# DeltaNet on one core: head results transposed behind later projections, gates ahead of projections, pieces of products between the last merges

## The chip, the cores and the metric

The kernel runs on one core of a Trainium2 chip. The metric is the device time of one execution in microseconds (us). One execution was also recorded by the hardware profiler; line numbers such as L1378 are lines of the kernel before unless the text says that they are of the changed one. Engines: PE multiplies matrices, DVE works on vectors, ACT on functions and copies, POOL is the third elementwise engine, SP issues the DMAs.

## The reference, cut to what matters

The program is two blocks of a network on 256 tokens with a context of 256 more. The change lies in one layer, a gated delta rule ("DeltaNet") with 8 key heads, each with 2 value heads, in two directions of time:

```python
def project(h):
    p = h @ w_in
    qkv = silu(short_conv_2(p[..., :DN_QKV_DIM], conv_w))
    z = p[..., DN_QKV_DIM:DN_QKV_DIM + DN_V_DIM]
...
def step(s, xs):                       # gated_delta_rule, one chunk
    m = where(strict, bc[..., :, None] * kk * decay, 0.0)
    sol = triangular_solve(eye + m, rhs, lower=True, unit_diagonal=True)
...
def readout(o, z):
    o = rms_norm_2(swapaxes(o, 1, 2), norm_g)
    o = o * silu(z.reshape(bsz_, n, DN_V_HEADS, DN_HEAD_V))
    return o.reshape(bsz_, n, DN_V_DIM) @ w_out
```

So each head needs four projections (q and k in one tile, two value parts), two gates `z`, the inverse of a unit triangular matrix, a recurrence over chunks, a normalised and gated result, and a product with its part of `w_out`.

## The kernel before, in words

Everything of this layer is in the function `deltanet`. All products with weights take three matmuls per 128 input channels (`mm3`, L310 to L318): weight and activation are each split in a high and a low part, and high by high, high by low and low by high are added in PSUM. A weight of 1024 by 128 therefore makes 24 matmuls of 512 columns. `weight` (L298) loads it by DMA, ACT casts the high part (L307), POOL in this layer subtracts to get the low part (L308).

The pieces of a head are:
- `project(hd)` (L1140): four products of 24 matmuls. ACT and DVE apply a convolution of 5 taps straight from PSUM (L1148, L1153), ACT a SiLU.
- `gates(hd)` (L1159): two products of 24 matmuls, which only ACT reads, with a SiLU, into `z`.
- `prepare(hd)` (L1169): transposes of k, products of k and q (L1200), decay products (L1209, L1210) that ACT exponentiates into `D` (L1214), and `Mt`. `Mt` goes through DRAM (`din`), DVE inverts blocks of 16 by substitution (L1239, L1240), ACT copies (`XX`, L1241), and the blocks go through DRAM (`dout`, L1247) into `TT` (L1255).
- `tokens` (L1259): transposes of q and of two value tiles.
- `merge(hd)` (L1282): three levels of two halves, each of three groups of four 128-column products (L1297, L1303, L1308) with a copy by ACT (L1294) and DVE work between, which grow the blocks of the inverse to 128.
- `steps(hd)` (L1312): four steps of two directions, with the results in two tiles `ot`.
- `readout` (L1367): ACT squares `ot` (L1372), DVE takes an inverse square root by integer guess and three rounds (`rsqrt`, L416 to L422) and scales `ot` (L1378); PE transposes `ot` in two groups of four (L436, called from `transpose`), DVE multiplies by `z` (L1384), and `pair` splits the product into high and low parts (L294, L295).
- `write_out(hd)` (L1388): eight products of 6 matmuls, whose results DVE adds to the tokens (`finish`, L641).

A scheduler of the framework sets the order of instructions of each engine from the order in which the code issues them and from their dependences; each engine then runs its own list in order. `issue_after(x)` puts all PE instructions of its block behind the instruction x in PE's list. The main loop (L1409) is a software pipeline: while head hd goes through its steps, the preparation of hd+1 and the projections of hd+2 are on their way. PSUM has eight banks, which this layer shares as three rings (L1801): `b` for transposes and preparation, `a` for merges and steps, `mm` for products with weights.

## Time and profile before

| what | value |
|---|---|
| three runs, us | 2682.57, 2691.01, 2696.7 (median 2691.01) |
| profiled execution, us | 2684.89 |
| its span, us | 2683.1 |
| busy share of the span | PE 94%, PEld (weight loads of PE) 79%, DVE 61%, ACT 42%, POOL 14% |
| mean granted clock of TensorE | 0.971 of full speed |
| DMA | 334.09 MB, mean 125 GB/s |

The median is of separate runs; the trace belongs to the profiled execution, whose span is 1.8 us shorter than its device time. A row of a timeline gives the start in us from the start of the span, the duration, the engine, the line, what was written from what, the sizes, how many instructions were put together, and in brackets how long the engine had stood idle before and what released it. The DeltaNet layer is in the middle of the span; a matmul of PE is pipelined, so that one of 0.39 us can be followed by the next after 0.23 us.

### The profile page before, as it was taken

What the parts mean: (1) busy time and instruction counts of PE and PEld (TensorE: products, weight loads), DVE (VectorE), ACT (ScalarE), POOL (GpSimd) and SP (SyncE); (2) the same over time, 40 slices, a digit from 0 to 9 for tenths busy, and PEclk for the clock granted to TensorE, in tenths of its full rate; (3) what the DMA queues carried; (4) which work ended last, traced back from release to release, by engine and by line L of the source; (5) the groups of instructions that cost most, each with busy time, mean ns of one, the idle gap of its engine ahead of it and who ended that gap; (6) DMA issues with size and microseconds to landing.
All of it is one profiled execution on the core that took longest, in us unless ns stands there. A gap on an engine that the chain in (4) does not pass through costs nothing.

```text
span 2683.1 us, 40564 instructions
## 1 busy us (share of the span) xinstructions
PE 2515.0 (94%) x15740; PEld 2117.8 (79%) x15740; DVE 1640.5 (61%) x3455; ACT 1133.2 (42%) x2159; POOL 363.2 (14%) x268
## 2 busy tenths in 40 slices
PE   7999999999999899879899989987999999798999
PEld 4866877778887899757787778776877888698999
DVE  4554443334576778777866786776533435777675
ACT  3344333222454455544444444433422324564453
POOL 0000200000100100232223323222000001410100
PEclk8999999999999899889999999999999999899999
DMA  7334476662241565222112211211544522231554
GB/s 263 124 121 141 165 276 243 237 241 87 82 128 60 169 192 182 72 58 59 35 51 63 58 48 54 64 43 48 195 162 169 181 91 71 77 95 58 179 182 157
DMA packets 147105, 334.09 MB, mean 125 GB/s; under 512 B 57134, under 2 KB 68512, under 8 KB 146912
## 3 DMA queue, kind: packets, MB, share of 16 engines
q1 hardware_dynamic: 146656, 331.43, 37.9%
q8 instruction: 124, 2.03, 0.3%
q14 instruction: 69, 0.57, 0.1%
q0 software_dynamic: 256, 0.07, 0.0%
HBM read 327.78 MB, written 3.67 MB: 124 GB/s over the span
## 4 chain that ended last, share of the span: by engine, by line
PE 74%; DVE 16%; ACT 3%; issue 3%; DMA 2%; POOL 1%; SPq 1%; DVEq 0%; POOLq 0%; ACTq 0%
PE pmm L316 18%; PE pmm L317 17%; PE pmm L318 17%; PE pmd L378 3%; DVE lf L1239 2%; PE ps L986 1%; PE pa L1303 1%; PE pmm L335 1%; DVE wl L308 1%; DVE rsy L422 1%; DMA wm<-wmod 1%; PE pa L1350 1%; PE pmm L336 1%; PE pmm L334 1%; PE pv L1024 1%
## 5 line engine op out<-in xcount | busy, mean ns | idle before, releaser
L307 ACT CAST wh<-wr 128x1024 fp32r<-128x1024 f32 (+1 forms) x421 | 426.4, 1017 | 740.7 <-PE pmm L317 537.6
L316 PE MATMUL pmm<-h,wh 128*128 128x512 f32 (+2 forms) x1800 | 630.7, 350 | 25.0 <-DVE kq L1153 13.9
L318 PE MATMUL pmm<-h,wl 128*128 128x512 f32 (+2 forms) x1800 | 626.4, 348 | 16.5 <-DVE wl L308 12.1
L317 PE MATMUL pmm<-h,wh 128*128 128x512 f32 (+2 forms) x1800 | 625.1, 347 | 0.0
L308 DVE TENSOR_TENSOR wl<-wr,wh 128x1024 fp32r<-128x1024 f32 (+1 forms) x333 | 394.7, 1187 | 302.2 <-ACT wh L307 295.7
L316 PE MATMUL pmm<-r,wh 128*128 128x256 f32 (+1 forms) x1312 | 445.1, 340 | 7.2 <-DVE rst L420 3.9
L318 PE MATMUL pmm<-r,wl 128*128 128x256 f32 (+1 forms) x1312 | 444.9, 340 | 5.4 <-DVE wl L308 5.3
L317 PE MATMUL pmm<-r,wh 128*128 128x256 f32 (+1 forms) x1312 | 445.7, 340 | 2.2 <-DVE r L295 2.1
L308 POOL TENSOR_TENSOR wl<-wr,wh 128x1024 fp32r<-128x1024 f32 x88 | 214.2, 2437 | 1428.4 <-ACT wh L307 817.0
L316 PEld LDWEIGHTS pmm<-h,wh 128*128 128x128 f32 x1800 | 348.0, 193 | 74.4 <-issue 24.3
L318 PEld LDWEIGHTS pmm<-h,wl 128*128 128x128 f32 x1800 | 348.5, 194 | 59.8 <-DVE wl L308 13.3
L317 PEld LDWEIGHTS pmm<-h,wh 128*128 128x128 f32 x1800 | 348.8, 194 | 37.2
L316 PEld LDWEIGHTS pmm<-r,wh 128*128 128x128 f32 x1312 | 248.7, 190 | 41.2 <-issue 13.2
L318 PEld LDWEIGHTS pmm<-r,wl 128*128 128x128 f32 x1312 | 249.3, 190 | 32.2 <-DVE wl L308 6.7
L317 PEld LDWEIGHTS pmm<-r,wh 128*128 128x128 f32 x1312 | 249.6, 190 | 26.2 <-DVE r L295 2.8
L641 DVE SCALAR_TENSOR_TENSOR xs<-pmm,modb,xs 128x256 f32<-128x256 f32 x232 | 106.3, 478 | 135.1 <-PE pmm L318 134.9
L641 DVE SCALAR_TENSOR_TENSOR xs<-pmm,moda,xs 128x256 f32<-128x256 f32 x120 | 54.4, 480 | 149.0 <-PE pmm L318 148.9
L294 ACT CAST r<-h 128x256 fp32r<-128x256 f32 (+1 forms) x128 | 65.6, 514 | 127.0 <-DVE h L594 67.3
L295 DVE TENSOR_TENSOR r<-h,r 128x256 fp32r<-128x256 f32 (+1 forms) x128 | 72.9, 570 | 43.3 <-ACT r L294 39.9
L378 PE MATMUL pmd<-wm,cvs 128*32 128x256 f32 x1408 | 87.7, 384 | 0.3 <-DMA wm<-wmod 0.3
L378 PEld LDWEIGHTS pmd<-wm,cvs 128*32 128x32 f32 x1408 | 41.2, 110 | 40.7 <-issue 14.2
L334 PE MATMUL pmm<-h,wh 128*128 128x256 f32 x224 | 64.6, 295 | 5.4 <-ACT h L499 3.5
(483 smaller groups left out, 3784.9 us busy)
## 6 DMA issues: line engine op xcount, KB each, us to landing
wr<-w SPq DMA_DIRECT2D x128, 512.0 KB
wr<-f SPq DMA_DIRECT2D x128, 512.0 KB
wm<-amod SPq DMA_DIRECT2D x24, 2048.0 KB
wr<-dwin SPq DMA_DIRECT2D x49, 512.0 KB
wm<-wmod SPq DMA_DIRECT2D x12, 2048.0 KB
wr<-win SPq DMA_DIRECT2D x28, 512.0 KB
wm<-wmod SPq DMA_DIRECT2D x8, 1536.0 KB
wr<-gwin SPq DMA_DIRECT2D x17, 512.0 KB
```

What stands on the lines that cost most here:

```text
L294: self.nc.scalar.copy(hi, src)
L295: self.nc.vector.tensor_tensor(lo, src, hi.bitcast(F32), ALU.subtract)
L307: self.nc.scalar.copy(hi, raw)
L308: (self.nc.gpsimd if pool or self.pool_lo else self.nc.vector).tensor_tensor(lo, raw, hi.bitcast(F32), ALU.subtract)
L316: mm(ps, wh[:, k, :], rh[:, n0:n1], start=k == 0, stop=False)
L317: mm(ps, wh[:, k, :], rl[:, n0:n1], start=False, stop=False)
L318: mm(ps, wl[:, k, :], rh[:, n0:n1], start=False, stop=k == last)
L334: mm(ps[:, c0:c1], wh[:, k, :], rh[:, c0:c1], start=k == 0, stop=False)
L335: mm(ps[:, c0:c1], wh[:, k, :], rl[:, c0:c1], start=False, stop=False)
L378: self.last = nc.tensor.matmul(ps[32 * c : 32 * c + 32, :256], cs[:, k + i, :], raw[:, i, 256 * c : 256 * c + 256], start=k + i == 0, stop ...
L641: self.nc.vector.scalar_tensor_tensor(x, ps, mod[:, 8 * gch + m, v : v + 1], x, ALU.mult, ALU.add)
L1239: nc.vector.tensor_tensor(p3, N3[:, i : i + 1, 0:i].to_broadcast([P, i, i]), X[:, 0:i, 0:i].rearrange("p j c -> p c j"), ALU.mult)
```

## The change

The change has four parts.

1. `readout` is cut in two. `scale` (squares, square root, scaling of `ot`) is called where `readout` was; the rest, from the transposes on, is called after `project(hd + 2)`, and `issue_after` puts it behind the last matmul of that projection. For head 6, which has no such projection, it stands behind the first gate product of head 7, for head 7 behind the last pieces of part 3.
2. `gates(0)` comes ahead of `tokens` and `project(1)`.
3. For head 7 the second gate product and the whole of `write_out(6)` become 24 pieces of 3 matmuls (`lin_parts`, `late`). `between` issues one piece behind the first product group of each of the six half levels of the merge and behind each direction of steps 0 to 2, two behind each direction of step 3, and the rest follows the steps.
4. The PSUM rings change from b=3, a=3, mm=2 to b=2, a=3, mm=3.

```diff
--- before.py
+++ after.py
@@ -315,13 +315,29 @@
         for k, (rh, rl) in list(enumerate(rhs))[k0:k1]:
             mm(ps, wh[:, k, :], rh[:, n0:n1], start=k == 0, stop=False)
             mm(ps, wh[:, k, :], rl[:, n0:n1], start=False, stop=False)
-            mm(ps, wl[:, k, :], rh[:, n0:n1], start=False, stop=k == last)
+            self.mark = mm(ps, wl[:, k, :], rh[:, n0:n1], start=False, stop=k == last)
 
     def lin(self, src, rhs, n0, n1, w=None, pool=False):
         w = w or self.weight(src, pool=pool)
         ps = self.mm_ps()
         self.mm3(ps[:, : n1 - n0], w, rhs, n0, n1)
         return ps[:, : n1 - n0]
+
+
+    def lin_parts(self, w, rhs, n, use):
+        ps = self.mm_ps()[:, :n]
+        w = w()
+        for k in range(len(rhs)):
+            yield lambda: self.mm3(ps, w, rhs, 0, n, k, k + 1)
+        use(ps)
+
+    def between(self, parts, ins, n=1):
+        for _ in range(n):
+            part = next(parts, None)
+            if part is None:
+                return
+            with self.tc.issue_after(ins):
+                part()
 
 
     def lins(self, ws, rhs, streams, tag="mm"):
@@ -1156,14 +1172,32 @@
                     vf.append(acc)
             return kq, vf
 
+
+        def gate(hd, j):
+            ps = self.lin(win[5 + 6 * hd + j], h, 0, 512)
+            z = ap.tile([P, 512], F32, tag="z" if hd < 7 else "vf", bufs=2, name="z")
+            nc.scalar.activation(z, ps, AF.Silu)
+            return z
+
         def gates(hd):
-            zs = []
-            for j in range(2):
-                ps = self.lin(win[5 + 6 * hd + j], h, 0, 512)
-                z = ap.tile([P, 512], F32, tag="z", bufs=2, name="z")
-                nc.scalar.activation(z, ps, AF.Silu)
-                zs.append(z)
-            return zs
+            return [gate(hd, 0), gate(hd, 1)]
+
+
+        def late(zs, og):
+            def use(ps):
+                zs.append(ap.tile([P, 512], F32, tag="vf", bufs=2, name="z"))
+                nc.scalar.activation(zs[1], ps, AF.Silu)
+
+            yield from self.lin_parts(lambda: self.weight(win[48]), h, 512, use)
+            ws = [self.weight(a["dwout"][6, mq]) for mq in range(2)]
+            for m in range(8):
+                c = slice(P * (m % 4), P * (m % 4) + P)
+
+                def use(ps):
+                    for s2 in st:
+                        self.finish(xs, m, ps[:, s2[0] : s2[1]], mod, 2, s2, None, None)
+
+                yield from self.lin_parts(lambda: [w[:, :, c] for w in ws[m // 4]], og, 512, use)
 
         junk = lambda: ap.tile([P, P], F32, tag="junk", bufs=1, name="junk")
 
@@ -1279,7 +1313,7 @@
             c["vt"] = vt
 
 
-        def merge(hd, c):
+        def merge(hd, c, parts):
             Mt, TT = c["Mt"], c["TT"]
 
             def mix(t, p, np_, s):
@@ -1294,7 +1328,8 @@
                     nc.scalar.copy(v4(FT), mix(TT[1], 4 * hf, 4, s))
                     py = self.a_ps()
                     for p in range(4):
-                        mm(py[:, C(p)], Mt[:, 2 * hf + p // 2, p % 2], mix(TT[0], 4 * hf + p, 1, s), start=True, stop=True)
+                        i = mm(py[:, C(p)], Mt[:, 2 * hf + p // 2, p % 2], mix(TT[0], 4 * hf + p, 1, s), start=True, stop=True)
+                    self.between(parts, i.ins)
                     Y = ap.tile([P, 512], F32, tag="Y", bufs=2, name="Y")
                     nc.vector.tensor_tensor(Y.rearrange("p (a i) -> p a i", a=4), py.rearrange("p (a i) -> p a i", a=4),
                                             lm[:, lv].unsqueeze(1).to_broadcast([P, 4, P]), ALU.mult)
@@ -1305,11 +1340,11 @@
                         nc.vector.tensor_tensor(o, o, v4(py), ALU.subtract)
                     pzt = self.a_ps()
                     for p in range(4):
-                        mm(pzt[:, C(p)], Y[:, C(p)], FT[:, C(p)], start=True, stop=True)
+                        i = mm(pzt[:, C(p)], Y[:, C(p)], FT[:, C(p)], start=True, stop=True)
                     nc.vector.tensor_tensor(mix(TT[1], 4 * hf, 4, s), v4(FT), v4(pzt), ALU.subtract)
 
 
-        def steps(hd, c):
+        def steps(hd, c, parts):
             kq, vt, D, mbt, ktm, TB = c["kq"], c["vt"], c["D"], c["mbt"], c["ktm"], c["TT"][1]
             S = None
             ot = [ap.tile([P, 512], F32, tag="ot", bufs=2, name="ot") for _ in range(2)]
@@ -1347,7 +1382,8 @@
                     if step:
                         mm(pks[:, 256:], ks(1), S[:, 256 * d : 256 * d + 256], start=True, stop=True)
                     for v in range(2):
-                        self.mark = mm(ptr[:, 256 + P * v : 384 + P * v], D[ch][:, 2 * d + v], vA[:, C(v)], start=True, stop=True)
+                        i = mm(ptr[:, 256 + P * v : 384 + P * v], D[ch][:, 2 * d + v], vA[:, C(v)], start=True, stop=True)
+                    self.between(parts, i.ins, 2 if step == 3 else 1)
                     o = ot[ch // 2][:, 256 * (ch % 2) : 256 * (ch % 2) + 256]
                     if step:
                         tq = self.e()
@@ -1364,7 +1400,7 @@
                 S = Sn
             return ot
 
-        def readout(c, ot, zs):
+        def scale(c, ot):
             ss = sp.tile([P, 4, 2], F32, tag="ss", name="ss")
             jk = junk()
             for ch in range(4):
@@ -1376,6 +1412,8 @@
             for p in range(2):
                 o = ot[p].rearrange("p (c i) -> p c i", i=P)
                 nc.vector.tensor_tensor(o, o, so[:, 4 * p : 4 * p + 4].unsqueeze(2).to_broadcast([P, 4, P]), ALU.mult)
+
+        def readout(ot, zs):
             og = []
             for v in range(2):
                 pt = self.b_ps()
@@ -1402,29 +1440,36 @@
                     then(sv)
 
         c = prepare(0, *project(0))
+        zs = gates(0)
         tokens(c)
         proj = project(1)
-        zs = gates(0)
-        og = None
+        og, parts = None, iter(())
         for hd in range(8):
-            merge(hd, c)
-            ot = steps(hd, c)
             if hd == 7:
-                zs = gates(hd)
+                parts = late(zs, og)
+            merge(hd, c, parts)
+            ot = steps(hd, c, parts)
             if hd < 7:
                 nxt = prepare(hd + 1, *proj)
-            if hd == 7:
-                with self.tc.issue_after(self.mark.ins):
-                    write_out(6, og)
-            elif hd > 0:
+            if 0 < hd < 7:
                 write_out(hd - 1, og)
             if hd < 7:
                 tokens(nxt)
-            og = readout(c, ot, zs)
+            scale(c, ot)
+
             if hd < 6:
                 proj = project(hd + 2)
+            elif hd == 6:
+                zn = [gate(7, 0)]
+            else:
+                for part in parts:
+                    part()
+            with self.tc.issue_after(self.mark.ins):
+                og = readout(ot, zs)
             if hd < 6:
                 zs = gates(hd + 1)
+            elif hd == 6:
+                zs = zn
             if hd < 7:
                 c = nxt
         S = dict(acc={}, new=lambda n: ap.tile([P, 512], F32, tag="FT", bufs=2, name="acc")[:, :n],
@@ -1798,7 +1843,7 @@
                 f = dict(h=self.norm_mod(xs, both, gs, mods2[0][0], 0, [y[:, :2], y[:, 2:]], "sq", self.hr()),
                          ws=[self.weight(a["dwin"][m]) for m in range(2)])
         with ExitStack() as st:
-            self.pools(st, dict(g=3, e=(5, 256)), dict(b=3, a=3, mm=2), 4, "b", pool_lo=True)
+            self.pools(st, dict(g=3, e=(5, 256)), dict(b=2, a=3, mm=3), 4, "b", pool_lo=True)
             self.dn = st.enter_context(self.tc.tile_pool(name="dn", bufs=1))
             h = self.deltanet(xs, mods2[0][0], f["h"], f["ws"], [both[0], both[1]] if skip else [both[1], both[0]])
         S = {}
```

The lists of PE show where instructions go. The lines of the changed kernel are other numbers: L452 is L436 of before, L1331, L1338 and L1343 are L1297, L1303 and L1308, and L316 to L318 are the same. Names: `pmm<-h` is a projection or gate product, `pmm<-r` one of `write_out`, `pb<-k_id,ot` a transpose of the result, `pa<-TT,Mt` the first group of a half level of a merge.

PE at the end of head 1, before. The 31 projection matmuls of which the last four stand here follow the last transposes of `vf`:

```order
L316 MATMUL pmm<-h,wh 128x512
L317 MATMUL pmm<-h,wh 128x512
L318 MATMUL pmm<-h,wl 128x512
L316 MATMUL pmm<-h,wh 128x512
L436 MATMUL pb<-k_id,ot 128x128 x4
L317 MATMUL pmm<-h,wh 128x512
L436 MATMUL pb<-k_id,ot 128x128 x4
L318 MATMUL pmm<-h,wl 128x512
L316 MATMUL pmm<-h,wh 128x512
```

The same place, changed:

```order
L316 MATMUL pmm<-h,wh 128x512
L317 MATMUL pmm<-h,wh 128x512
L318 MATMUL pmm<-h,wl 128x512
L452 MATMUL pb<-k_id,ot 128x128 x8
L316 MATMUL pmm<-h,wh 128x512
L317 MATMUL pmm<-h,wh 128x512
L318 MATMUL pmm<-h,wl 128x512
L316 MATMUL pmm<-h,wh 128x512
```

What moved: the two groups of four transposes are eight in a row, and 96 projection matmuls instead of 31 stand between them and the steps.

PE between steps(0) and merge(1), before. Behind the steps come 55 projection and gate matmuls, the transposes of `ot`, and 15 more, of which the last three stand here:

```order
L316 MATMUL pmm<-h,wh 128x512
L317 MATMUL pmm<-h,wh 128x512
L318 MATMUL pmm<-h,wl 128x512
L1297 MATMUL pa<-TT,Mt 128x128 x4
L436 MATMUL pb<-k_id,kq 128x128 x4
L1200 MATMUL pb<-kq 128x256
L1303 MATMUL pa<-Y,FT 128x128 x4
L1308 MATMUL pa<-FT,Y 128x128 x4
```

The same place, changed. Behind the steps come 10 matmuls, of which the last three stand here:

```order
L316 MATMUL pmm<-h,wh 128x512
L317 MATMUL pmm<-h,wh 128x512
L318 MATMUL pmm<-h,wl 128x512
L1331 MATMUL pa<-TT,Mt 128x128 x4
L1338 MATMUL pa<-Y,FT 128x128 x4
L1343 MATMUL pa<-FT,Y 128x128 x4
L1331 MATMUL pa<-TT,Mt 128x128 x4
L1338 MATMUL pa<-Y,FT 128x128 x4
L1343 MATMUL pa<-FT,Y 128x128 x4
L1331 MATMUL pa<-TT,Mt 128x128 x4
L452 MATMUL pb<-k_id,ot 128x128 x8
L1338 MATMUL pa<-Y,FT 128x128 x4
```

What moved: 60 of the 70 matmuls went ahead, most of them to before merge(0), and the transposes of `ot` now stand inside merge(1).

PE at the start of merge(7), before. Ahead of it are 48 gate matmuls, with the transposes of `ot` behind the first 31:

```order
L316 MATMUL pmm<-h,wh 128x512
L317 MATMUL pmm<-h,wh 128x512
L318 MATMUL pmm<-h,wl 128x512
L1297 MATMUL pa<-TT,Mt 128x128 x4
L1303 MATMUL pa<-Y,FT 128x128 x4
L1308 MATMUL pa<-FT,Y 128x128 x4
L1297 MATMUL pa<-TT,Mt 128x128 x4
L1303 MATMUL pa<-Y,FT 128x128 x4
L1308 MATMUL pa<-FT,Y 128x128 x4
```

The same place, changed. Ahead of the transposes are 24 gate matmuls:

```order
L317 MATMUL pmm<-h,wh 128x512
L318 MATMUL pmm<-h,wl 128x512
L452 MATMUL pb<-k_id,ot 128x128 x8
L1331 MATMUL pa<-TT,Mt 128x128 x4
L316 MATMUL pmm<-h,wh 128x512
L317 MATMUL pmm<-h,wh 128x512
L318 MATMUL pmm<-h,wl 128x512
L1338 MATMUL pa<-Y,FT 128x128 x4
L1343 MATMUL pa<-FT,Y 128x128 x4
L1331 MATMUL pa<-TT,Mt 128x128 x4
L316 MATMUL pmm<-h,wh 128x512
L317 MATMUL pmm<-h,wh 128x512
```

What moved: a piece of three gate matmuls follows the first product group of each half level, and `ot` is transposed right ahead of the merge.

## Rows read from the trace of the kernel before

**Rows 1.** The page, part 4, shares by engine.
```profile
PE 74%; DVE 16%; ACT 3%; issue 3%; DMA 2%; POOL 1%; SPq 1%; DVEq 0%; POOLq 0%; ACTq 0%
```

**Rows 2.** Stretches: length, busy us of PE, PEld, DVE, ACT, POOL, clock, DMA, GB/s.
```profile
1333.30:1425.20 91.90, 83.94 (x485) 70.13 (x484) 67.85 (x164) 41.97 (x105) 28.40 (x16) 0.98 0.20 54
1423.40:1427.10 3.70, 3.69 (x14) 3.22 (x15) 2.90 (x5) 0.86 (x2) 0.00 (x0) 0.55 0.76 169
1452.00:1477.00 25.00, 23.62 (x192) 20.85 (x190) 18.85 (x46) 12.76 (x37) 9.30 (x8) 1.00 0.11 36
1797.60:1820.00 22.40, 16.08 (x129) 14.78 (x127) 10.46 (x16) 4.94 (x8) 2.35 (x1) 1.00 0.10 27
```

**Rows 3.** Waits of PE, one head: total us, times, longest.
```profile
PE pb L436 <- DVE ot L1378: 4.6, 1, 4.6
PE pa L1350 <- DVE S L1343: 1.7, 1, 1.7
```

**Rows 4.** Timeline of PE, head 2: start, us, line, operation, [idle before <- releaser].
```profile
1411.49 0.48 PE L316 MATMUL pmm<-h,wh 128*128 128x512 f32 x1
...
1418.41 0.39 PE L316 MATMUL pmm<-h,wh 128*128 128x512 f32 x1
1423.41 1.12 PE L436 MATMUL pb<-k_id,ot 128*128 128x128 f32 x4 [4.62 <-DVE ot L1378]
...
1427.07 0.39 PE L316 MATMUL pmm<-h,wh 128*128 128x512 f32 x1
```

**Rows 5.** Timeline of DVE, same place.
```profile
1420.31 2.32 DVE L422 SCALAR_TENSOR_TENSOR rsy<-rst,rsy 128x8 f32<-128x8 f32 x1
1422.67 1.29 DVE L1378 TENSOR_TENSOR ot<-ot,rsy 128x512 f32<-128x512 f32 x2
```

**Rows 6.** Timeline, a weight of the same place on ACT and POOL.
```profile
1419.15 1.04 ACT L307 CAST wh<-wr 128x1024 fp32r<-128x1024 f32 x1
...
1420.27 2.34 POOL L308 TENSOR_TENSOR wl<-wr,wh 128x1024 fp32r<-128x1024 f32 x1 [5.58 <-ACT wh L307]
```

**Rows 7.** Timeline of SP and PE: TT comes back, and its first reader.
```profile
1423.13 7.83 SPq L1255 DMA_DIRECT2D TT<-dout  x16
...
1452.02 1.05 PE L1297 MATMUL pa<-TT,Mt 128*128 128x128 f32 x8
```

**Rows 8.** Groups of ACT in one head: busy us, mean ns, idle before.
```profile
L1214 ACT ACTIVATE D<-pb,nG 128x128 f32<-128x128 f32 x16 | 4.5, 384 | 0.0
...
L1294 ACT COPY FT<-TT 128x512 f32<-128x512 f32 x6 | 3.4, 616 | 5.1 <-DVE TT L1309 5.1
...
L1214 ACT ACT_TABLE_LOAD x1 | 1.3, 1283 | 0.0
...
L1267 ACT ACTIVATE junk<-pb 128x128 f32<-128x128 f32 x4 | 1.1, 279 | 5.3 <-PE pb L436 5.2
...
L1267 ACT ACTIVATION_READ_ACCUMULATOR junk<-pb 128x1 f32 x4 | 0.8, 196 | 0.0
```

**Rows 9.** Timeline of PE, start: projection(1), merge(0), end of steps(0), merge(1).
```profile
1161.00 0.77 PE L316 MATMUL pmm<-h,wh 128*128 128x512 f32 x1 [13.55 <-DVE kq L1153]
...
1190.36 1.05 PE L1297 MATMUL pa<-TT,Mt 128*128 128x128 f32 x8
...
1247.65 0.71 PE L1350 MATMUL pa<-e,D 128*128 128x128 f32 x4
...
1267.98 1.05 PE L1297 MATMUL pa<-TT,Mt 128*128 128x128 f32 x8
```

**Rows 10.** Timeline of PE and SP, head 6 to the end.
```profile
1790.54 1.11 PE L436 MATMUL pb<-k_id,ot 128*128 128x128 f32 x4 [4.61 <-DVE ot L1378]
...
1800.41 0.82 PE L1303 MATMUL pa<-Y,FT 128*128 128x128 f32 x5 [1.73 <-ACT FT L1294]
...
1859.71 0.66 PE L436 MATMUL pb<-k_id,ot 128*128 128x128 f32 x4 [0.89 <-DVE ot L1378]
...
1790.26 7.98 SPq L1255 DMA_DIRECT2D TT<-dout  x16
```

## The prediction

> **What bounds the kernel now.** I read the profile from the outside in. The chain that ended last lies on PE for 74% and on DVE for 16% of the span [rows 1], so what counts is time in which PE stands still, or runs at its lower clock, while something else is late. The diff touches the DeltaNet stage alone, where one head follows another. In a window of one head PE is busy 83.94 of 91.90 us, DVE 67.85, ACT 41.97 [rows 2]: the reader is to see that PE is the bound and that no other engine is near it.
>
> What PE waits for in such a head is nearly one thing: 4.6 us, once, before the transposes of `ot`, for DVE's scaling at L1378; nothing else is above 1.7 us [rows 3]. The timeline shows the place in head 2: 31 projection matmuls from 1411.49 to 1418.41, one each 0.23 us (6.92 / 30), then nothing until 1423.41 [rows 4]. The same wait stands in each of heads 1 to 6 (six in all, the last at 1790.54 with 4.61 us [rows 10]), 91.8 us apart ((1790.54 − 1423.41) / 4). Behind it the granted clock of 1423.40:1427.10 is 0.55, so mostly the lower level of 1.2 GHz [rows 2]; the first matmul at full pace starts at 1427.07 [rows 4]. That loses another 3.7 × (1 − 0.55) = 1.6 us. A head therefore loses 4.6 + 1.6 = **6.2 us** at this place.
>
> `ot` is late because DVE works through the next head's substitution and the square root side by side; one of its 8-column operations takes 2.32 us while POOL subtracts a weight [rows 5, 6], and the scaling comes at 1422.67. None of that changes. What changes is what PE does meanwhile.
>
> **The change, part by part.**
>
> *Transposes behind the projections, heads 1 to 5.* Before, 31 projection matmuls stand between the last token transposes and `ot`'s; now 96, or 22 us by 0.23. `ot` is ready 12.5 us after the first of them (1411.49 to 1422.67 + 1.29), so the wait and the slow restart go: −6.2 us a head. The vector work behind the transposes (z, hi and lo) comes later too, but its readers, `write_out`'s matmuls, stand in the next steps. The other chain past this point, through the substitution and DRAM to TT, doesn't lie on PE: its DMAs are issued by 1430.96, and the merge that reads TT starts at 1452.02 [rows 7]. Of these 21 us a head that is 6 us shorter leaves 15.
>
> What the change gives back per head shows nowhere in the trace of before, so it is bounded:
> - With two b buffers instead of three, the third group of token transposes waits until ACT has squared the first: 1.1 + 0.8 us [rows 8], with 6 matmuls (1.4 us) between. 0 to 1.9; I take 1.0, as ACT may have a copy ahead.
> - The projections run without a pause, so their weights are wanted sooner. A cast took 1.04 and a subtraction 2.34 us [rows 6]. 0 to 3.4; I take 0.4, since each weight serves 24 matmuls (5.5 us).
> - In the merges the decay products use the b ring, which ACT empties by L1214 in fours, 1.1 us each (4.5 / 4) [rows 8]. With a buffer less up to two fills wait: 0 to 2.3; I take 0.3, because the fills lie apart between merge products.
> - Convolutions behind a third mm buffer, and transposes that wait for a b buffer: 0 to 0.6; I take 0.3.
>
> They add to 2.0 (0 to 8.2, but much over 5 needs all at once). Net −4.2 a head, −1 to −6.2; five heads make **−21 (−31 to −5)**.
>
> Short waits between merge products could also cost clock. The trace has such a stretch: in 1797.60:1820.00 PE is busy only 16.08 of 22.40 us, and the granted clock is 1.00; in 1452:1477, with 23.62 of 25 us busy, it is also 1.00 [rows 2]. So I add nothing. The Trainium skill, "TensorE: Matmul & The Clock Gate", section "A second HAM failure mode: psum-queue depth-cycling", says otherwise of a kernel that cycles through PSUM banks: small pauses between groups made the clock swing between its levels and lowered throughput. By that rule the sum would be that of the last rival below; the trace does not agree so far.
>
> *Start: gates before projections.* Before, 218 projection and gate matmuls stand ahead of merge(0), now 275; behind steps(0) stood 70, now 10. PE idles 13.55 us up to 1161.00, as project(1)'s third group wants a PSUM buffer that DVE's convolution still reads [rows 9]. The 48 gate matmuls (11 us) need ACT alone to empty them, and there are three mm buffers: they fill that hole. At the other end steps(0) ends at 1248.4 (1247.65 + 0.71), and merge(1) starts at 1267.98, 19.6 us later [rows 9]; behind 10 matmuls it can start after 2.3: −17.3. Against it, 57 more matmuls (13 us) stand ahead of merge(0), which starts at 1190.36 [rows 9], and convolutions of project(1) now mix with head 0's substitution on DVE. It may start 0 to 13 us later; I take 3.3, a quarter, as the hole nearly holds them. **−14 (−17 to −4).**
>
> *Head 6 to 7 and the end.* `ot`(6) now comes behind 24 gate matmuls, fewer than before, so PE waits for it longer; but merge(7) isn't held by that: its TT is issued from 1790.26 to 1798.24, and PE waits 1.73 us for ACT's copy of it at 1800.41 [rows 10]. That chain is the same, so no gain; a restart at the lower clock adds 1.6 us, as above (0 to 3.2). Of the 72 late matmuls 18 go into the merges (4.1 us, where PE idled 6.3 of 22.4 [rows 2]), 24 into the steps (5.5 us, partly in pauses: 0 to 5.5, I take 0), and 30 stay behind them instead of 48, 4.1 us less. But `ot`(7) then decides: its second transposes waited 0.89 us until 1859.71 [rows 10] for DVE, which had 16 accumulations of `write_out`(6) among the square root's operations. Six of them go ahead of it now, so it gets part of the 4.1 us that the matmuls save: 0 to 4.1, I take 2.6, about two thirds, since the square root itself doesn't change. 1.6 − 2.6 = **−1 (−4 to +6)**.
>
> *Sum.* −21 − 14 − 1 = −36. The profiled execution took 2684.89 us, 6.1 below the median of 2691.01; on its own scale that gives 2648.9, against the median **2655**.
>
> **The rivals.**
> 1. *The wait only moves* (20%). PE, set free, meets the next late thing: a weight, a convolution, a buffer. For it: a weight takes 3.4 us after its cast begins [rows 6], and POOL's subtractions stretch DVE's work. Against: DVE and ACT have 24 and 50 us to spare in a head [rows 2]. Heads give −1 each: −5 − 14 − 1 = −20, so 2671.
> 2. *The start gains little* (12%), since merge(0) slips by nearly all of its 13 us: −21 − 4 − 1 = −26, so 2665.
> 3. *The change does not do what it says* (12%): both of these, −5 − 4 − 1 = −10, so 2681, or 2688 with the bad end of the last term.
> 4. *Slower: the b ring puts ACT on PE's path in the merges* (5%). PE takes its instructions in order, so a decay product that waits for ACT holds the merge products behind it. If ACT's work there comes to stand in line, it is L1214 4.5, its table load 1.3 and L1294 3.4 = 9.2 us a head [rows 8]; over six heads 55, less 36: +19, so 2710. It decides from 6 us a head (36 / 6). Against it: ACT is busy 12.76 of 25 us in that stage [rows 2].
> 5. *Slower: the clock falls in the merges* (3%). If half of a stage of 25 us ran at the 0.55 seen behind the wait, it took 12.5 × (1 / 0.55 − 1) = 10 us more a head: 60 − 36 = +24, so 2715. Rows 2 speak against it. The page named above would have this happen.
>
> **How the numbers follow.** The forecast has 48%. The range goes down to all terms at their good ends (−31 − 17 − 4 = −52, counted from the fastest run shown, 2682.57: 2630) and up to rival 3 at 2688; rivals 4 and 5 and some tails stay outside: **2630 to 2688**. A difference below 0.5% (13 us) can hardly be told from none here. Faster by more: forecast and rivals 1 and 2, less 4% for their upper parts, 76%. The same: rival 3 and these 4%, 16%. Slower: 8%.
>
> **What would show it.** Right: the 4.6 us for `ot` is gone from PE's waits in heads 1 to 5, the period of the transposes falls from 91.8 to about 87.6 us, the 13.55 us for `kq` is gone, and merge(1) starts within 5 us of the end of steps(0). Wrong: PE's waits in a head add up to as much under other names, with a period above 90 us; merge(0) starts later than 1200; the granted clock in the merges is below 0.9; or `ot`(7) is transposed later than 18 us behind the last step.

## The result, and the profile after

The changed kernel took 2655.14 us (median of four runs, 2649.31 to 2661.69), the kernel before 2687.40 us (four runs) beside it: a ratio of 0.9877 with a 95% interval of 0.9837 to 0.9916. The forecast was 2655. The profiled execution of the changed kernel has a span of 2647.5 us, 35.6 less than before; 36 were forecast on that scale.

Most of this document splits these 35.6 us into stages. To compare traces whose starts differ, every stage is measured inside the layer: from its first product (the first matmul of 256 columns that reads `h`, at 1082.16 us before, 1078.44 after), over the first products of merge(1), merge(2), merge(6) and merge(7), the first and the last product of steps(7), and the last transposes of `ot`(7), to the matmul of `write_out`(7) from which on it keeps its full pace (0.28 to 0.29 us each). All are rows of PE's timeline.

| stage, us | before | after | difference | forecast |
|---|---|---|---|---|
| first product to merge(1) | 185.8 | 177.3 | −8.5 | −14 |
| merge(1) to merge(6), five heads | 459.3 | 431.9 | −27.4 | −21 |
| merge(6) to merge(7) | 70.4 | 69.4 | −1.0 | |
| merge(7) | 23.0 | 27.8 | +4.8 | |
| steps(7) | 20.9 | 26.6 | +5.7 | |
| last step to full pace | 29.0 | 24.0 | −5.0 | |
| the four of the end together | 143.3 | 147.7 | +4.4 | −1 |
| sum in the layer | 788.4 | 757.0 | −31.5 | −36 |
| outside it | 1894.7 | 1890.6 | −4.1 | 0 |

The last row is code that is the same in both. Over the 14 traces of this study it lies between 1890.6 and 1900.5 us, and 3.7 of the 4.1 us lie ahead of the layer, so they belong to no part of the change, and spans of single executions are only good to some 10 us. The sum in the layer repeats better: the changed kernel, profiled again on another chip, has 757.8. The place of "full pace" depends on where PE last had to wait: counted to the last matmul of `write_out`(7) instead (1879.79 us before, 1845.67 after), the layer gains 30.4 us.

In the profile after, first stretches: one head, merge(7) and steps(7) (columns as in [rows 2]).

```profile
1429.40:1515.50 86.10, 82.40 (x485) 69.02 (x484) 68.85 (x164) 41.73 (x105) 28.63 (x16) 1.00 0.22 58
1757.00:1784.80 27.80, 23.44 (x146) 20.13 (x146) 11.02 (x16) 3.42 (x6) 0.00 (x0) 0.88 0.05 5
1784.80:1811.40 26.60, 23.49 (x125) 18.14 (x126) 14.17 (x41) 9.80 (x27) 2.35 (x1) 1.00 0.06 21
```

A head is 5.8 us shorter, its granted clock is 1.00 instead of 0.98, and PE's busy time for the same 485 matmuls falls by 1.5 us, which goes with not running at the lower level. What PE waits for in that head:

```profile
PE pa L1367 <- DVE e L1363: 1.6, 1, 1.6
PE pa L1343 <- DVE Y L1334: 1.0, 1, 1.0
...
PE pb L452 <- ACT junk L1301: 0.2, 1, 0.2
```

The line of 4.6 us [rows 3] is gone and no line of its size has come. The 0.2 us are the third group of token transposes behind ACT's squares, the first give-back of the forecast. Now PE's timeline at merge(0), at the end of steps(0) and merge(1), at `ot` of head 3, at head 6 to 7, and at the end:

```profile
1197.49 1.05 PE L1331 MATMUL pa<-TT,Mt 128*128 128x128 f32 x8
...
1252.95 0.67 PE L1385 MATMUL pa<-e,D 128*128 128x128 f32 x4
...
1255.77 0.94 PE L1331 MATMUL pa<-TT,Mt 128*128 128x128 f32 x7
...
1503.73 1.03 PE L452 MATMUL pb<-k_id,ot 128*128 128x128 f32 x8
...
1751.69 1.94 PE L452 MATMUL pb<-k_id,ot 128*128 128x128 f32 x8 [5.90 <-DVE ot L1414]
1757.02 2.04 PE L1331 MATMUL pa<-TT,Mt 128*128 128x128 f32 x8 [3.39 <-DMA TT<-dout]
...
1829.35 1.97 PE L452 MATMUL pb<-k_id,ot 128*128 128x128 f32 x8 [11.11 <-DVE ot L1414]
```

Merge(1) starts 2.1 us behind steps(0) (1252.95 + 0.67), 19.6 before [rows 9]; merge(0) starts 119.0 us behind the first product instead of 108.2. The eight transposes of a head start without a wait. At the end PE waits 5.90 us for `ot`(6), 3.39 us for TT, and 11.11 us for `ot`(7): these are the waits that answer to [rows 10].

### The profile page after: what moved, and what is told of

It is laid out like the page before. It is cut to its first block, busy times and chain, and to the rows that moved or that the text cites. A ratio compares the mean times of both kernels' runs of the same rounds, so it can differ in the third digit from the quotient of the medians.

```text
span 2647.5 us, 40581 instructions
## 1 busy us (share of the span) xinstructions
PE 2502.9 (95%) x15740; PEld 2108.2 (80%) x15740; DVE 1651.0 (62%) x3455; ACT 1134.0 (43%) x2161; POOL 365.6 (14%) x268
## 5 line engine op out<-in xcount | busy, mean ns | idle before, releaser
L318 PE MATMUL pmm<-h,wl 128*128 128x512 f32 (+2 forms) x1800 | 623.9, 347 | 18.2 <-DVE wl L308 9.9
L316 PE MATMUL pmm<-h,wh 128*128 128x512 f32 (+2 forms) x1800 | 628.8, 349 | 7.4 <-ACT wh L307 1.9
L316 PE MATMUL pmm<-r,wh 128*128 128x256 f32 (+1 forms) x1312 | 444.3, 340 | 3.2 <-DVE q L987 1.6
L318 PE MATMUL pmm<-r,wl 128*128 128x256 f32 (+1 forms) x1312 | 443.5, 339 | 3.3 <-DVE wl L308 3.2
L318 PEld LDWEIGHTS pmm<-h,wl 128*128 128x128 f32 x1800 | 346.1, 192 | 61.0 <-DVE wl L308 11.1
L316 PEld LDWEIGHTS pmm<-h,wh 128*128 128x128 f32 x1800 | 345.8, 192 | 53.8 <-issue 7.2
L316 PEld LDWEIGHTS pmm<-r,wh 128*128 128x128 f32 x1312 | 247.8, 189 | 37.2 <-issue 8.9
L318 PEld LDWEIGHTS pmm<-r,wl 128*128 128x128 f32 x1312 | 248.2, 189 | 29.6 <-DVE wl L308 4.5
L657 DVE SCALAR_TENSOR_TENSOR xs<-pmm,moda,xs 128x256 f32<-128x256 f32 x120 | 54.4, 479 | 147.7 <-PE pmm L318 147.5
L295 DVE TENSOR_TENSOR r<-h,r 128x256 fp32r<-128x256 f32 (+1 forms) x128 | 72.8, 569 | 43.5 <-ACT r L294 39.9
L1369 ACT COPY e<-pa 128x256 f32<-128x256 f32 x64 | 23.8, 371 | 128.9 <-PE pa L1367 128.4
```

The source lines that it names most:

```text
L295: self.nc.vector.tensor_tensor(lo, src, hi.bitcast(F32), ALU.subtract)
L316: mm(ps, wh[:, k, :], rh[:, n0:n1], start=k == 0, stop=False)
L318: self.mark = mm(ps, wl[:, k, :], rh[:, n0:n1], start=False, stop=k == last)
L657: self.nc.vector.scalar_tensor_tensor(x, ps, mod[:, 8 * gch + m, v : v + 1], x, ALU.mult, ALU.add)
L1369: nc.scalar.copy(vA, ptr[:, :256])
```

## The experiments

The trace left a question that the agreement of the totals hides: which part does what? Four kernels each take one part out of the changed kernel. All stages are measured as above; "period" is the mean of the four between merge(2) and merge(6), "end" is from merge(6) to full pace.

| kernel | ratio to before (95%) | to merge(2) | period | end | sum in the layer |
|---|---|---|---|---|---|
| before | | 277.7 | 91.85 | 143.3 | 788.4 |
| changed | 0.9877 (0.9837 to 0.9916) | 264.9 | 86.07 | 147.7 | 757.0 |
| e1, rings of before | 1.0021 (1.0011 to 1.0031) | 273.6 | 92.42 | 148.8 | 792.1 |
| e2, transposes back | 1.0007 (0.9998 to 1.0017) | 272.9 | 92.05 | 150.8 | 791.9 |
| e3, gates back | 0.9902 (0.9887 to 0.9917) | 266.5 | 86.14 | 149.7 | 760.8 |
| e4, late pieces off | 0.9879 (0.9863 to 0.9896) | 266.8 | 86.12 | 143.7 | 755.0 |
| e5, rings and transposes alone | 0.9870 (0.9853 to 0.9887) | 265.3 | 86.12 | 144.8 | 754.6 |
| e6, pieces in the merges only | 0.9857 (0.9829 to 0.9885) | 266.0 | 86.12 | 143.8 | 754.3 |
| e7, low parts on DVE | 0.9877 (0.9856 to 0.9899) | 265.6 | 86.11 | 143.7 | 753.8 |
| e8, e6 and e7 | 0.9840 (0.9819 to 0.9860) | 266.4 | 86.12 | 137.2 | 748.1 |
| e9, transposes half way | one run | 267.4 | 87.17 | 148.7 | 764.8 |
| f1, changed again | 0.9887 (0.9870 to 0.9903) | 266.0 | 86.12 | 147.3 | 757.8 |
| f2, e8 again | 0.9860 (0.9845 to 0.9874) | 265.2 | 86.12 | 140.0 | 749.8 |
| f3, e8 and two more low parts | 0.9846 (0.9829 to 0.9863) | 265.0 | 86.12 | 137.4 | 746.9 |

### e1: the PSUM rings back

```diff
-            self.pools(st, dict(g=3, e=(5, 256)), dict(b=2, a=3, mm=3), 4, "b", pool_lo=True)
+            self.pools(st, dict(g=3, e=(5, 256)), dict(b=3, a=3, mm=2), 4, "b", pool_lo=True)
```

> The changed kernel with the PSUM rings of before (b=3, mm=2). My theory is that the heads gain from the moved transposes alone, and that the third mm buffer matters only at the start: the period of a head stays at 85 to 87 us, no wait for ot above 1 us; behind steps(0) PE now has 43 projection matmuls instead of 10, so merge(1) comes some 7.5 us (33 x 0.228) later, and the span is 2650 to 2660 (changed kernel 2647.5). The rival is that the third mm buffer lets PE run ahead while it waits and gives most of the gain in the heads: then the period goes back above 89 us and the span above 2665. A third reading, that one b buffer less costs PE waits in every merge, gives a period below 85 and a span below 2645.

The period went to 92.42 us and the ratio to 1.0021: one line that names three numbers takes away the whole gain. PE's waits in one head of e1, and the place in the timelines of PE and DVE in another head:

```profile
PE pmm L316 <- DVE kq L1169: 4.6, 1, 4.6
PE pa L1385 <- DVE S L1378: 1.0, 1, 1.0
```

```profile
1517.69 0.47 PE L316 MATMUL pmm<-h,wh 128*128 128x512 f32 x1 [4.52 <-DVE kq L1169]
...
1530.30 1.03 PE L452 MATMUL pb<-k_id,ot 128*128 128x128 f32 x8
```

```profile
1513.24 1.29 DVE L1414 TENSOR_TENSOR ot<-ot,rsy 128x512 f32<-128x512 f32 x2
1514.46 3.09 DVE L1169 SCALAR_TENSOR_TENSOR kq<-pmm,dcw,kq 128x508 f32<-128x508 f32 x4
```

The wait for `ot` is gone as in the changed kernel, and a wait of the same 4.6 us stands 17 matmuls further, behind 48 instead of 31: the third projection product wants a PSUM buffer, and both are still unread, since the convolution that reads the first (L1169 is L1153 of before) stands behind the scaling in DVE's list. The last step ends at 1500.88; the scaling ends 13.6 us behind it, the convolution 16.7. This is the first rival of the forecast, in the kernel without the third buffer. In the changed kernel, whose last step ends at 1480.16, the same convolution ends 16.9 us behind it, and the first matmul that needs its buffer, the 73rd of the projection, starts at 1498.29:

```profile
1493.96 3.08 DVE L1169 SCALAR_TENSOR_TENSOR kq<-pmm,dcw,kq 128x508 f32<-128x508 f32 x4
1498.29 0.39 PE L316 MATMUL pmm<-h,wh 128*128 128x512 f32 x1
```

So the third buffer is enough by 1.2 us. In e1 merge(1) comes 183.7 us behind the first product, 6.4 later than in the changed kernel, about as I had it, but my expectation that the third buffer matters at the start alone falls.

### e2: the transposes back

```diff
             scale(c, ot)
+            if hd < 6:
+                og = readout(ot, zs)
...
-            with self.tc.issue_after(self.mark.ins):
-                og = readout(ot, zs)
+            if hd >= 6:
+                with self.tc.issue_after(self.mark.ins):
+                    og = readout(ot, zs)
```

> The changed kernel with the transposes of heads 0 to 5 issued where they were before, right behind the scaling. My theory: the wait for ot comes back with 4 to 6 us in heads 1 to 5, with the lower clock behind it, the period goes back to 91 to 93 us and the span to 2671 to 2683 (2647.5 + 5 x 5 to 7). The rival, that the rings or the other parts made the gain in the heads: the period stays below 88 and the span below 2655.

The period is 92.05 us, the ratio 1.0007. In one head of e2:

```profile
PE pb L452 <- DVE ot L1414: 4.1, 1, 4.1
PE pa L1367 <- DVE e L1363: 1.6, 1, 1.6
```

So in the heads the ring alone gives nothing either: the wait for `ot` is back with 4.1 us, behind 32 projection matmuls. The span, 2684.6 us, is 1.6 above the range that I had. The two parts are not two gains that add; each removes one of two places at which PE meets the same late DVE, and PE gets past only when both are gone.

### e3: gates(0) back behind tokens(0) and project(1)

```diff
         c = prepare(0, *project(0))
-        zs = gates(0)
         tokens(c)
         proj = project(1)
+        zs = gates(0)
```

> The changed kernel with gates(0) behind tokens(0) and project(1) as before. My theory: PE has no work again while DVE reads project(1) out of PSUM, the idle time ahead of merge(0) grows by 5 to 10 us, and 28 matmuls instead of 10 stand behind steps(0) (18 x 0.228 = 4.1 us): merge(1) comes 6 to 12 us later than in the changed kernel, span 2653 to 2660. The rival is that the third mm buffer fills the hole by itself: then merge(1) comes 0 to 4 us later, span below 2652. Periods of the heads unchanged in both, 86 us.

Merge(1) came 174.4 us behind the first product, 2.9 sooner than in the changed kernel (177.3), and merge(2) 1.6 later: neither theory had merge(1) come sooner. The span, 2658.9 us, lies in my range only because 7.5 of its 11.4 us over the changed kernel fell outside the layer. PE's waits between 1120 and 1200 us, e3 and then the changed kernel:

```profile
PE pmm L316 <- DVE kq L1169: 9.4, 1, 9.4
PE pb L1243 <- ACT g L1237: 4.5, 1, 4.5
PE pb L1243 <- DVE row L1150: 2.2, 1, 2.2
```

```profile
PE pb L452 <- DVE vt L1310: 4.3, 1, 4.3
PE pmm L318 <- POOL wl L308: 3.6, 1, 3.6
PE pb L1243 <- ACT g L1237: 3.2, 1, 3.2
PE pb L1243 <- DVE row L1150: 2.1, 1, 2.1
```

The hole of 13.6 us [rows 9] is 9.4 in e3 and gone in the changed kernel, as forecast, but 4.3 and 3.6 us for other things stand in its place. What merge(1) gained came with the ring: with three mm buffers the scheduler itself leaves 28 matmuls behind steps(0) where 70 stood, while e1, which has the moved gates and two buffers, needs 183.7 us to merge(1). The order of the gates is worth 1.6 us at merge(2), which is no more than the scatter there (264.9 to 266.8 in kernels that are the same up to that point).

### e4: no late pieces

```diff
-            if hd == 7:
-                parts = late(zs, og)
...
-                zn = [gate(7, 0)]
+                zn = gates(7)
             else:
-                for part in parts:
-                    part()
+                with self.tc.issue_after(self.last):
+                    write_out(6, og)
```

> The changed kernel without the late pieces: both gate products of head 7 (48 matmuls) behind steps(6) ahead of the transposes of ot, write_out(6) whole (48 matmuls) behind steps(7). My theory after the trace: the pieces lie on the chain of merge(7) and steps(7), which took 54.4 us with them and 43.9 before; without them these two go back to 43 to 45 us, the clock ahead of merge(7) stays up since PE has 5.5 us more work there, and the 48 matmuls (10.9 us) fit into the 17.9 us between the last step and the transposes of ot(7). Span 2635 to 2640. The rival is that DVE's accumulations, now all behind the steps, hold up the scaling of ot(7), so that the transposes come 22 to 28 us behind the last step: span 2642 to 2650, no gain.

Merge(7) and steps(7) of e4 as stretches:

```profile
1760.60:1787.90 27.30, 19.47 (x128) 18.13 (x128) 11.01 (x16) 3.41 (x6) 0.00 (x0) 0.82 0.11 24
1787.90:1808.90 21.00, 19.06 (x101) 13.73 (x102) 11.56 (x35) 8.30 (x25) 0.00 (x0) 1.00 0.00 1
```

Merge(7) of e5, then of e8, two kernels that follow below:

```profile
1761.35:1785.12 23.77, 16.05 (x130) 14.79 (x128) 11.04 (x16) 4.94 (x8) 2.34 (x1) 1.00 0.10 26
1757.21:1782.00 24.79, 21.80 (x147) 18.49 (x147) 13.65 (x22) 3.42 (x6) 0.00 (x0) 0.94 0.12 27
```

Steps(7) go back to 20.9 us: the 24 matmuls in the steps (24 × 0.228 = 5.5 us) cost the changed kernel their full time. Merge(7) does not go back to 23.0: it takes 27.3 us without any piece in it, at a granted clock of 0.82, so there the pieces are free, and the 4 to 5 us more than before go with the lower clock behind PE's idle time (PE still waits 3.62 us for TT). The length follows the clock: 23.8 us at 1.00 in e5, where PE has work ahead of it, 24.8 at 0.93 to 0.94 in e8 and f3, 27.0 to 27.3 at 0.82 to 0.83 in e4, e6 and f2. My expectation that a fuller PE ahead of it keeps the clock up was wrong, as long as the last 3.6 us are idle. The second transposes of `ot`(7) came 16.7 us behind the last step, not 22 to 28, so the rival's reason falls too. The end is 4.0 us shorter than in the changed kernel; the span, 2648.2 us, and the ratio, 0.9879, can't be told from those of the changed kernel.

### e5: two parts alone

The kernel before with the rings and the moved transposes of heads 0 to 5, nothing else:

```diff
+                with self.tc.issue_after(self.last.ins):
+                    og = readout(ot, zs)
...
-            self.pools(st, dict(g=3, e=(5, 256)), dict(b=3, a=3, mm=2), 4, "b", pool_lo=True)
+            self.pools(st, dict(g=3, e=(5, 256)), dict(b=2, a=3, mm=3), 4, "b", pool_lo=True)
```

> The kernel before with two of the four parts alone: the PSUM rings (b=2, mm=3) and the transposes of heads 0 to 5 behind the projections. Gates(0), the gates of head 7 and write_out(6) stay as before. My theory after the first four runs is that these two together, and neither alone, carry the gain of the heads and of the start: period 86 us, merge(2) 264 to 268 us behind the first product of the layer (changed kernel 264.9, before 277.7), span 2645 to 2656. The rival is that the other two parts carry a third or more of it: span 2660 or above.

The sum in the layer is 754.6 us, the ratio 0.9870: the two parts are enough, and the gates and the late pieces together add nothing that the runs can tell. In e5 15 gate matmuls stand between the transposes of `ot`(6) and merge(7), which then takes 23.8 us: with PE at work ahead of it the slow start of 4 to 5 us is nearly gone.

### e6, e7, e8: what the end hangs on

In the changed kernel PE waits 11.11 us for the scaling of `ot`(7). DVE and POOL at that place:

```profile
1819.68 2.00 DVE L438 SCALAR_TENSOR_TENSOR rsy<-rst,rsy 128x8 f32<-128x8 f32 x1
1821.72 2.26 DVE L436 TENSOR_TENSOR rst<-rsy 128x8 f32<-128x8 f32 x1
1824.01 2.26 DVE L437 TENSOR_TENSOR rst<-rst,rsh 128x8 f32<-128x8 f32 x1
1826.31 2.26 DVE L438 SCALAR_TENSOR_TENSOR rsy<-rst,rsy 128x8 f32<-128x8 f32 x1
1828.61 1.29 DVE L1414 TENSOR_TENSOR ot<-ot,rsy 128x512 f32<-128x512 f32 x2
```

```profile
1819.31 9.24 POOL L308 TENSOR_TENSOR wl<-wr,wh 128x1024 fp32r<-128x1024 f32 x4 [2.17 <-ACT wh L307]
```

Four operations on 8 columns, which take 0.17 us elsewhere in the same chain, take 2.00 to 2.26 us each, one after another, while POOL subtracts four weights: three of the next feed-forward layer and, as e7 shows, one of `write_out`(7). Each ends 0.02 to 0.03 us behind the subtraction beside it. Before, two were caught (2.38 and 2.26 us), and from the last step to the transposes it was 18.2 us before and 17.9 after, so the time won was lost there. That the late pieces let those weights follow each other sooner fits, but is not shown: without the pieces two operations are caught in e4 and three in e5. The Trainium skill, "SBUF — State Buffer", section "Who interferes with whom", says that a VectorE instruction with two inputs in SBUF contends with a GpSimd instruction that reads SBUF. These rows agree with it.

e6 puts pieces into the merges only:

```diff
-                    self.between(parts, i.ins, 2 if step == 3 else 1)
+                    self.last = i.ins
...
-                zn = [gate(7, 0)]
+                zn = gates(7)
             else:
-                for part in parts:
-                    part()
+                self.between(parts, self.last, 24)
```

> The changed kernel with both gate products of head 7 ahead of the transposes of ot, pieces of write_out(6) in the six half levels of merge(7) only, none in the steps, and the other 30 matmuls behind the last step. My theory: pieces in the merges cost nothing (27.8 us with them, 27.3 without), pieces in the steps cost their own 5.5 us; so merge(7) takes 27 to 28 us, steps(7) 21 us instead of 26.6, and what is left fits the wait for ot(7): span 2640 to 2645 against 2647.5. The rival is that the end hangs on the scaling of ot(7) by DVE, which then only waits longer: transposes of ot(7) 20 us or more behind the last step, span 2645 to 2650.

Steps(7) took 20.9 us and merge(7) 27.2, as the theory had it; 18.1 us from the last step to the transposes stayed, so the scaling comes no sooner, though not later either, as the rival had it (20 us or more). The end is 3.9 us shorter than in the changed kernel, no more than without any pieces, and the span of 2652.5 us, above both ranges, shows nothing of it, with 7.7 us more outside the layer.

e7 is the changed kernel with the subtractions of the feed-forward layer's first four weights on DVE:

```diff
-            ws = [self.weight(self.a[w1][m], pool=True) for m in range(4)]
+            ws = [self.weight(self.a[w1][m], pool=w1 != "f1_0") for m in range(4)]
```

> The changed kernel with one edit behind the layer: the low parts of the first four weights of the next feed-forward layer are subtracted by DVE (1.19 us each in the trace of before) instead of POOL (2.4 us). In the changed kernel four 8-column operations of the square root of ot(7) took 2.00 to 2.26 us each instead of 0.17 while POOL subtracted those weights (9.24 us), and PE waited 11.11 us for the scaling. My theory: it is this collision; without it the scaling of ot(7) comes 3 to 8 us sooner, PE's wait is 3 to 8 us, the span 2639 to 2645. The rival: DVE takes its instructions in order, and the four subtractions (4.8 us) stand ahead of the square root, so that the wait stays at 9 to 14 us and the span at 2646 to 2652.

DVE and POOL of e7 at the same place:

```profile
1819.72 0.17 DVE L438 SCALAR_TENSOR_TENSOR rsy<-rst,rsy 128x8 f32<-128x8 f32 x1
1819.80 1.22 DVE L308 TENSOR_TENSOR wl<-wr,wh 128x1024 fp32r<-128x1024 f32 x1
1820.94 2.31 DVE L436 TENSOR_TENSOR rst<-rsy 128x8 f32<-128x8 f32 x1
...
1824.11 1.21 DVE L308 TENSOR_TENSOR wl<-wr,wh 128x1024 fp32r<-128x1024 f32 x1
...
1825.84 1.29 DVE L1414 TENSOR_TENSOR ot<-ot,rsy 128x512 f32<-128x512 f32 x2
```

```profile
1820.76 2.47 POOL L308 TENSOR_TENSOR wl<-wr,wh 128x1024 fp32r<-128x1024 f32 x1 [3.05 <-ACT wh L307]
```

POOL has one subtraction left in the chain, a weight of `write_out`(7), and one operation is caught, 2.31 us, at just that time; its neighbours take 0.17. PE's wait falls from 11.11 to 6.81 us, and the transposes come 13.7 us behind the last step. Some 4 of the 8 us are won back; two of the subtractions (1.2 us each) now stand on DVE between the operations of the root. The span, 2653.2 us, and the ratio, 0.9877, show no gain: the code outside the layer took 8.9 us longer, a place where this edit does nothing but move four subtractions; that is inside the scatter named above.

e8 has both edits:

> Both edits, of e6 and e7. If both theories hold they add: span 2632 to 2640, PE's wait for ot(7) below 6 us. If the end hangs on DVE alone, the result is that of the subtraction edit alone.

The end took 137.2 us: 10.5 less than in the changed kernel and 6.1 less than before. That is more than both alone (3.9 and 4.0), because merge(7) took 24.8 us; f2 below, the same kernel with a merge(7) of 27.0, has 140.0, which is 7.3 less than the changed kernel beside it. PE's wait for `ot`(7) was 6.86 us, so the part of the expectation that named a wait below 6 us was missed, and the span, 2641.2 us, lies just above the 2632 to 2640.

### e9: how far the transposes must move

```diff
-        def project(hd):
+        def project(hd, mid=None):
...
+                if j == 1 and mid:
+                    mid()
```

Here `mid` is the transposes, behind 48 projection matmuls instead of 96.

> The changed kernel with the transposes of heads 0 to 5 behind the second projection product (48 matmuls) instead of the fourth (96). My theory: all that the place has to do is to cover the time that DVE is late; ot was ready 13.4 us behind the last step with the transposes put back, and 48 matmuls with the token transposes last about 12.9 us. So PE waits 0 to 1 us for ot and the period stays at 86 to 87 us. The rival, that the transposes must stand clear of the projections, since their scaling and the convolutions share DVE: period 88 us or more, with a wait for kq or vf behind the transposes.

```profile
PE pa L1369 <- DVE e L1365: 1.6, 1, 1.6
...
PE pb L452 <- DVE ot L1416: 0.6, 1, 0.6
```

PE waits 0.6 us for `ot`, no wait for `kq` or `vf` shows, and the period is 87.17 us, just above the 86 to 87. With e2 and the changed kernel this is a series of three, all with three mm buffers: 32 projection matmuls of cover, 4.1 us of wait; 48 matmuls, 0.6; 96, none. What counts is how much work stands ahead of the transposes, measured against the 13.4 us by which the scaling comes behind the last step in e2 and e9. The whole head is 1.1 us longer than with 96, more than the wait; where the other 0.5 us go was not followed.

### f1, f2, f3: a version faster than both

All on one chip:

> The changed kernel itself, on the chip on which the next two run. Both theories: ratio to before 0.985 to 0.990, period of a head 86 us, PE waits 10 to 12 us for the scaling of ot(7).

> The kernel of e8 again (pieces in the merges only, low parts of the next layer's first four weights on DVE), beside the changed kernel. My theory, from the stages of e8 (748.1 us from the first product of the layer to full pace in the last product, changed kernel 757.0): 6 to 10 us faster than the changed kernel in the same chip's runs, ratio to before 0.982 to 0.986. The rival, that e8's 2642.76 us was a lucky chip: within 3 us of the changed kernel.

f3 adds this to e8, ahead of `write_out(7)`:

```diff
+        self.pool_lo = False
```

> The kernel of e8 with the low parts of write_out(7)'s two weights on DVE as well. In e8 one of the square root's operations still took 2.31 us while POOL subtracted one weight. My theory: it falls to 0.17 us, the subtraction costs DVE 1.2 us, ot(7) comes about 1 us sooner; span within 3 us of e8's. The rival: DVE's queue gets longer by the two subtractions ahead of the square root, ot(7) comes 1 to 3 us later.

The medians were 2657.77 us for the changed kernel, 2649.82 for e8 and 2645.36 for f3, beside 2687.66 before. The ratio of f3, 0.9846 (0.9829 to 0.9863), lies wholly below that of the changed kernel, 0.9887 (0.9870 to 0.9903); the one of e8, 0.9860 (0.9845 to 0.9874), overlaps with it by a hair. So f1 and f2 came out as my theories had them, f2 at the edge (8.0 us faster, ratio 0.9860). In f3 no operation of the square root is above 0.2 us, and PE waits 6.3 us for `ot`(7), 0.5 less than in f2. f3 has the shortest sum in the layer (746.9 us) and is faster than the changed kernel and than the kernel before; that it is faster than e8 is not shown, since their intervals overlap, and e8 had 0.9840 on another chip.

## Why the prediction was right, step by step

**The bound.** PE, and within it one wait of 4.6 us with a slow restart behind it, 6.2 us a head. The period fell by 5.8 us. That size was right, and so was the way of getting it: wait from one view, loss of clock from another. Which parts of the change bring it was not.

**Heads 1 to 5: −21 forecast, −27.4 measured,** inside the −31 to −5. The give-backs were put at 2.0 us a head and came to 0.4 (6.2 − 5.8): the third token transposes wait 0.2 us instead of 1.0, no wait for a weight shows, and the merges with one b buffer less have 1.0 us where 0.8 to 0.9 stood. But the step gave the wrong cause: it credited the moved transposes with all of it and let the third mm buffer in only as a cost of 0.3 us. e1 and e2 show that either part alone gives nothing in the heads. Had the change been the transposes alone, I would have forecast the same −21 and been wrong. The first rival described just this and was given 20%, without the condition that decides it: with two buffers PE can run 48 projection matmuls ahead of DVE, about 11 us, and DVE hands the first buffer back 16.7 us behind the last step.

**Start: −14 forecast, −8.5 at merge(1).** The hole of 13.55 us is gone and merge(1) follows steps(0) at once, both as forecast. Merge(0) came 10.9 us later behind the first product instead of 3.3, near the bad bound of 13; on the clock of the trace of before that is 1201.2, past the 1200 that was named as a sign of being wrong. And the cause was the ring again: without the moved gates (e3) merge(1) is no later, without the ring (e1) it gains 2.1 us.

**End: −1 forecast, +4.4 measured,** inside the −4 to +6. The restart of merge(7) at the lower clock was put at 1.6 us (0 to 3.2) and cost 4 to 5 (e4: 27.3 us without a piece, 23.0 before at full clock); a granted clock below 0.9 in a merge, another of the signs, did come there and nowhere else. The pieces in the steps were put at 0 of 5.5 us and cost all of it. The tail was put at −2.6 and gave −5.0 (−4.0 to the last matmul of `write_out`(7)), and not for the reason forecast: the forecast had the gain ahead of the transposes, but 0.2 us of it lie there and 4.8 behind them. POOL's subtractions had moved forward. After, they caught the square root four times instead of twice; before, they also caught the split behind the transposes (L295), and PE waited for that. Rows of before, and last the same split after:

```profile
1859.13 5.51 POOL L308 TENSOR_TENSOR wl<-wr,wh 128x1024 fp32r<-128x1024 f32 x2 [1.59 <-ACT wh L307]
1861.62 3.56 DVE L295 TENSOR_TENSOR r<-z,r 128x512 fp32r<-128x512 f32 x2
1865.24 0.58 PE L317 MATMUL pmm<-r,wh 128*128 128x256 f32 x1 [1.78 <-DVE r L295]
1832.37 1.35 DVE L295 TENSOR_TENSOR r<-z,r 128x512 fp32r<-128x512 f32 x2
```

**The sum.** −36 was forecast. The layer gave −31.5, and the span −35.6 by 4.1 us of scatter outside the layer, so part of the agreement is luck. So is the hit of 2655: it was counted from a median of 2691.01, which is 2687.40 with one more run, and the medians differ by 32.3 us. The interval of the ratio, 0.9837 to 0.9916, holds anything from −44 to −23 us.

**The other rivals.** The b ring did not put ACT on PE's path: the forecast's point was 6 us a head, and PE's waits in the merges rose by some tenths. The clock did not fall in the merges of a head; it is 1.00 over the whole head with b=2. The Trainium skill, "TensorE: Matmul & The Clock Gate", section "A second HAM failure mode: psum-queue depth-cycling", tells of a kernel whose clock swings as it cycles through PSUM banks; no run here shows that in a head. The two rivals that let the start or everything fail did not come about, though the start, at −8.5, lies midway between the forecast and its rival.

## What to carry to other kernels

When an engine waits for a late one, look for every place at which the two meet, not for the one that the profile names: the wait is shown at the first, and moving that work alone only brings the next into the rows, here with the same 4.6 us. Then count the cover in units of what the engine can do without the late one, PSUM buffers included: it has to exceed the lateness at each place (here 13.4 us for the transposes, 48 matmuls just short of it, 96 enough; 16.7 us for the first PSUM buffer, two buffers 4.5 us short, three enough by 1.2). And work put into the gaps of a dependent chain is free only where the gaps are longer than the work: three matmuls fitted the pauses of the merges and not those of the steps.

## What was not expected of the hardware

- DVE operations of the square root on 8 columns, with two inputs, took 2.00 to 2.40 us instead of 0.17 whenever they began during a weight's subtraction on POOL: all 72 such cases in the 14 traces, four in a row in the changed kernel; moving four subtractions to DVE, where they took 1.2 us each instead of 2.4, made the chain 4 us shorter though DVE had more to do.
- After an idle PE, merge(7), whose products wait for DVE between, took 26.4 to 27.8 us at a granted clock of 0.82 to 0.88 in ten kernels, against 23.0 at 1.00 before: the restart cost more than behind a wait with dense matmuls (1.6 us). In e8 and f3 merge(7) took 24.8 us at 0.93 to 0.94, in f2, which is e8 again, 27.0 at 0.83; why the clock came back sooner there is open.
- The same code outside the layer took 1890.6 to 1900.5 us in 14 executions (but for the few subtractions that e7 and its successors move), a scatter as large as several of the terms that were forecast.
